# Neighbourhood attention in a fixed order with scores one block ahead, K laid out contiguously, and later differences in two Strassen MLPs

## The chip, the cores and the metric

The kernel runs on one core of one Trainium2 chip. Its engines are TensorE (PE, matrix products, with its weight loads shown as PEld), VectorE (DVE), ScalarE (ACT), GpSimd (POOL) and SyncE (SP), which here issues nearly all DMAs. The metric is device time in microseconds (us) from start to end of one execution; a comparison uses the median of several runs. A profile is one further execution, taken by the hardware profiler; all its times are counted from the start of its span.

## The reference

A trunk of two residual layers over 1024 tokens of width 1024, in float32. Layer 0 is neighbourhood attention and an MLP; layer 1 is a gated DeltaNet and an MLP. The change touches the attention and the first product of both MLPs:

```python
def sq_relu_mlp(h, w1, w2):
    a = jax.nn.relu(h @ w1)
    return (a * a) @ w2                      # width 4096 between the two

def neighbourhood_attention(h, w_qkv, rpb, w_o):
    ...                                      # 16 heads of 64, token grid 16 rows x 64 columns
    qkv = (h @ w_qkv).reshape(B, rows, GRID_W, 3, H, dh)
    ...                                      # window of 8 rows x 16 columns around each query
    bias = rpb[:, drow[None, :, None, :, None], dcol[:, None, :, None, :]].astype(jnp.float32)
    s = jnp.einsum('brjchd,bnjkhd->bhjrcnk', qb, kb).astype(jnp.float32) * scale + bias
    p = jax.nn.softmax(jnp.where(mask, s, -jnp.inf), axis=(-2, -1)).astype(vb.dtype)
    o = jnp.einsum('bhjrcnk,bnjkhd->brjchd', p, vb)
    ...
    return (o @ w_o).astype(h.dtype)
```

## The kernel before

Dense products run in three passes: a float32 operand is split into a rounded part `hi` (a copy on ACT) and a remainder `lo` (a subtraction on DVE), and `hi*hi`, `hi*lo` and `lo*hi` are summed in one bank of PSUM. `split_w` (lines 122 to 128) does this for 4 x 128 x 128 weights, which `wraw` and a DMA on SP bring in. `product` (L147) is one output tile of 128 x 512: eight inner tiles, 24 matmuls.

**The attention.** `load_x` loads the tokens in an order that puts each strip of 8 columns x 16 rows together: block t is 128 tokens. It also makes V for all heads. `na` then goes through eight pairs of heads. For a pair it makes K and then Q, feature-major (128 features of two heads x 1024 tokens): for each half of the tokens a `product`, a scaling out of PSUM on DVE (L694), the `hi` parts on ACT (L696, L703), the `lo` parts on DVE and POOL (L699, L704), and DMAs from POOL's queue (L698, L705) that bring the parts of either head to the other 64 partitions. `khi` holds K's `hi` part; `ks` and `qs` hold, for each head, a `hi` and a `lo` part one above the other, so that scores take two matmuls: one on 64 rows (`qs` on `khi`) and one on 128 rows (`qs` on `ks`), both on L726.

The scores of a block reach over its own and the neighbouring blocks (`nb` is 3, or 2 at the edges), so they are 128 x 384 or 128 x 256. K is read with the index order (row, block, column), that is in runs of 8 columns, since the bias table `bias` is laid out as 16 rows x 56 columns. One DVE operation adds the bias, negates and takes the minimum (L729); ACT takes the exponential with its sum (L732), and writes it in the order (block, row, column); DVE takes the reciprocal and scales (L736, L737). PE transposes the probabilities (L740), the two heads' transposes are copied by ACT and DVE (L743, L745), and output products with V (L750) fill 64 columns for each head. `load_bias` fetches the table of a pair with 32 DMAs (L676), for the next pair into the other two of four buffers; the table in DRAM, `natab`, is made by `na_bias_table`.

The order of this stage is not fixed by the text: a scheduler orders each engine's instructions by priority and by when their operands come. The DeltaNet of layer 1 is different: it runs within `manual_schedule`, where every engine keeps the order of the text. What comes before and behind such a stretch can still be placed among its instructions.

**The MLPs** are one level of Strassen's scheme (seven products instead of eight). `mlp_first` goes through quads of two hidden tiles by two halves of the tokens; a quad is seven products of twelve matmuls each (L430), in the order 1, 5, 2, 6, 3, 7, 4. After a product, DVE forms its sums (L418), ACT applies ReLU and square (L406, L407), and the hidden tile goes to DRAM. `less` (L411 to L415) forms at once the four differences that the second product needs, two of them in place over a hidden tile that has just been stored, and stores them in `diff`. `split` (L381, L382) prepares the weights of the product after next. `square_sum` loads a half tile of the residual stream and, two products later, squares it for the norm. `mlp_second` and `Second` do the second product.

Of the kernel before, what the change touches and what calls it, by code (L numbers as in the profile page):

```python
# [37 lines left out]
class Trunk:  # L38
# [302 lines left out]
    def mlp_first(self, st, w1, get, spare, first, todo, second, moved):  # L341
# [45 lines left out]
        def quad(n):  # L387
# [23 lines left out]
            def less(i, out, x, y):  # L411

                if n < nq - 4:
                    nc.vector.tensor_tensor(out=out, in0=x, in1=y, op=ALU.subtract)
                    nc.sync.dma_start(out=self.diff[n, i], in_=out)  # L415

# [41 lines left out]
        quads, shared, s, sq, w = [quad(n) for n in range(nq)], {}, {}, {}, {}  # L458
# [11 lines left out]
        for m, (n, j) in enumerate(order):  # L470
# [81 lines left out]
    def na_bias_table(self, rpb):  # L552

        nc = self.nc
        tab = self.dram.tile([16, 8, 15, 56], FP32, name="natab")
        for g in range(2):
# [7 lines left out]
            for h in range(8):  # L564
                nc.sync.dma_start(out=tab[8 * g + h].rearrange("q r k -> r q k"), in_=e[15 * h:15 * h + 15])
# [95 lines left out]
    def na(self, st, v, wqkv, rpb):  # L661
# [4 lines left out]
        for i in range(4):  # L666
            b = self.work(f"bias{i}", [P, 16, 56])
# [3 lines left out]
        def load_bias(n):  # L671
            for hh in range(2):
                for r in range(16):
                    r0 = min(max(r - 4, 0), 8)
                    d0 = 7 + r0 - r
                    nc.sync.dma_start(out=bias[n % 2 * 2 + hh][r * 8:r * 8 + 8, r0:r0 + 8, :], in_=tab[2 * n + hh, :, d0:d0 + 8, :])  # L676

        load_bias(0)
        o = []
        for n in range(8):  # L680


            khi = self.work("qk2", dt=F32R)
            ks = [self.work("wvraw", bufs=2, dt=F32R) for _ in range(2)]
            qs = [self.work(f"qk{i}", dt=F32R) for i in range(2)]
            ab = slice(0, 64), slice(64, 128)
            for c0, scale in ((D, 1.0), (0, 0.125)):
                w = self.weight(wqkv[:, c0 + n * P:c0 + (n + 1) * P])
                full = self.work("qk3") if c0 else None
                for half in range(2):  # L690
                    sl = slice(half * HALF, (half + 1) * HALF)
                    ps = self.product(w, x, half)
                    f = full[:, sl] if c0 else self.half("r")
                    nc.vector.scalar_tensor_tensor(out=f, in0=ps, scalar=scale, in1=st["rstd", half], op0=ALU.mult, op1=ALU.mult)  # L694
                    if c0:
                        nc.scalar.copy(out=khi[:, sl], in_=f)  # L696
# [1247 lines left out]
```

## Time and profile before

| | us |
|---|---|
| median of 3 runs | 2745.16 (2743.61 to 2745.78) |
| the profiled execution | 2742.01 |
| its span, first to last instruction | 2740.3 |
| mean granted TensorE clock | 0.989 |
| attention, first score to last output product | 138.0 to 524.4 |
| first product of MLP 0, its matmuls (L430) | 604.6 to 930.8 |
| first product of MLP 1, its matmuls (L430) | 2042.1 to 2383.1 |

In the rows of the profile, `mm<-X,whi` means that the tile `mm` is written from `X` and `whi`. A row of a timeline has the start, the time, the engine, the line, the operation and how many neighbours were merged; in brackets stands the idle time before it and what ended it. Matmuls are pipelined: one lasts about 0.4 us, and the next begins long before that, so the cost of one is read from start to start, not from its duration. A row of a table of stretches has the length, then busy time and count for PE, PEld, DVE, ACT and POOL, then the granted clock, the DMA share and GB/s. A row of waits has the total, the count and the longest.

### The profile page before, as it was taken

What the parts mean: (1) busy time and instruction counts of PE and PEld (TensorE: products, weight loads), DVE (VectorE), ACT (ScalarE), POOL (GpSimd) and SP (SyncE); (2) the same over time, 40 slices, a digit from 0 to 9 for tenths busy, and PEclk for the clock granted to TensorE, in tenths of its full rate; (3) what the DMA queues carried; (4) which work ended last, traced back from release to release, by engine and by line L of the source; (5) the groups of instructions that cost most, each with busy time, mean ns of one, the idle gap of its engine ahead of it and who ended that gap; (6) DMA issues with size and microseconds to landing.
All of it is one profiled execution on the core that took longest, in us unless ns stands there. A gap on an engine that the chain in (4) does not pass through costs nothing. (4 is left out here: it accounts for less than half of the span.)

```text
span 2740.3 us, 40418 instructions
## 1 busy us (share of the span) xinstructions
PE 2636.6 (96%) x14172; PEld 2072.7 (76%) x14172; DVE 1834.1 (67%) x3407; ACT 1293.2 (47%) x2747; POOL 939.5 (34%) x1067
## 2 busy tenths in 40 slices
PE   8999999999999999999999999898988999999998
PEld 6766666677788887787777878787866788888776
DVE  5156555665665667975777887878576665567975
ACT  5134344435555654433445555555354455554444
POOL 0111101025433422542345555533324543432641
PEclk9999999999999999999999999999999999999999
DMA  7222212346554543333221222123366544553334
GB/s 193 54 49 51 65 43 52 90 145 217 175 171 138 189 157 124 99 115 101 50 48 41 53 55 51 38 49 105 114 212 194 189 156 165 171 165 118 108 108 142
DMA packets 322233, 312.48 MB, mean 114 GB/s; under 512 B 81518, under 2 KB 233710, under 8 KB 322030
## 3 DMA queue, kind: packets, MB, share of 16 engines
q1 hardware_dynamic: 313614, 301.43, 36.2%
q0 software_dynamic: 3072, 8.39, 1.4%
q8 instruction: 111, 1.82, 0.3%
q10 hardware_dynamic: 5344, 0.09, 0.1%
q14 instruction: 92, 0.75, 0.1%
HBM read 209.78 MB, written 91.66 MB: 110 GB/s over the span
## 5 line engine op out<-in xcount | busy, mean ns | idle before, releaser
L1615 PE MATMUL mm<-A,whi 128*128 128x512 f32 x1216 | 405.3, 414 | 1.1 <-DVE A L1615 1.1
L147 PE MATMUL mm<-X,whi 128*128 128x512 f32 x1024 | 337.9, 402 | 0.7 <-ACT X L757 0.7
L1615 PEld LDWEIGHTS mm<-A,whi 128*128 128x128 f32 x1216 | 215.0, 191 | 41.2 <-DVE A L1615 1.9
L1615 PE MATMUL mm<-A,wlo 128*128 128x512 f32 x608 | 241.5, 397 | 0.0
L147 PEld LDWEIGHTS mm<-X,whi 128*128 128x128 f32 x1024 | 190.6, 188 | 47.5 <-issue 7.5
L147 PE MATMUL mm<-X,wlo 128*128 128x512 f32 x512 | 205.8, 402 | 0.0
L1615 POOL TENSOR_TENSOR xt<-lp,xi 128x126 f32<-128x126 f32 (+22 forms) x248 | 110.0, 444 | 175.4 <-DMA lp<-dsc 156.6
L1615 DVE SCALAR_TENSOR_TENSOR X<-xp,cw,X 128x512 f32<-128x512 f32 x192 | 141.7, 778 | 1.7 <-ACT X L1615 1.0
L1615 PEld LDWEIGHTS mm<-A,wlo 128*128 128x128 f32 x608 | 115.4, 190 | 28.1
L382 DVE TENSOR_TENSOR wlo<-s,whi 128x512 fp32r<-128x512 f32 x112 | 91.2, 819 | 56.6 <-ACT whi L381 56.6
L406 ACT ACTIVATE r<-r 128x512 f32<-128x512 f32 x120 | 75.7, 631 | 105.2 <-DVE r L418 105.1
L127 ACT CAST whi<-wraw 128x512 fp32r<-128x512 f32 (+1 forms) x110 | 66.0, 603 | 113.4 <-PE mm L147 77.2
L1615 POOL TENSOR_TENSOR xi<-xi,xt 128x126 f32<-128x126 f32 (+22 forms) x248 | 112.0, 451 | 19.4
L147 PEld LDWEIGHTS mm<-X,wlo 128*128 128x128 f32 x512 | 96.4, 188 | 20.6 <-issue 1.7
L128 DVE TENSOR_TENSOR wlo<-wraw,whi 128x512 fp32r<-128x512 f32 (+1 forms) x110 | 93.4, 851 | 27.0 <-ACT whi L127 26.9
L147 PE MATMUL mm<-A,whi 128*128 128x512 f32 (+1 forms) x336 | 105.7, 396 | 5.8 <-DVE hr L316 3.3
L1591 PE MATMUL mm<-X,whi 128*128 128x512 f32 x336 | 105.9, 396 | 0.0
L1591 PE MATMUL mm<-A,whi 128*128 128x512 f32 x336 | 105.9, 396 | 0.0
L1591 PE MATMUL pq<-X,whi 128*128 128x512 f32 x336 | 105.7, 396 | 0.0
L1591 PE MATMUL pq<-A,whi 128*128 128x512 f32 x336 | 105.7, 396 | 0.0
L698 POOL DMA_DIRECT2D wvraw<-qk x32 | 17.2, 540 | 247.0 <-ACT qk L696 240.4
L430 PE MATMUL pq<-X,whi 128*128 128x512 f32 x304 | 97.2, 401 | 0.0
(441 smaller groups left out, 7051.7 us busy)
## 6 DMA issues: line engine op xcount, KB each, us to landing
quad<-in_mlp_w_dram SPq DMA_DIRECT2D x60, 512.0 KB
hidden<-r SPq DMA_DIRECT2D x120, 256.0 KB
diff<-r SPq DMA_DIRECT2D x66, 256.0 KB
wraw<-in_gdn_w_in_dram SPq DMA_DIRECT2D x64, 256.0 KB
X<-in_mlp_w_dram SPq DMA_DIRECT2D x26, 512.0 KB
wraw<-in_mlp_w_dram SPq DMA_DIRECT2D x52, 256.0 KB
A<-in_mlp_w_dram SPq DMA_DIRECT2D x26, 512.0 KB
X<-diff SPq DMA_DIRECT2D x48, 256.0 KB
```

What stands on the lines that cost most here:

```text
L127: nc.scalar.copy(out=hi[:, :nk], in_=raw[:, :nk])
L128: nc.vector.tensor_tensor(out=lo[:, :nk], in0=raw[:, :nk], in1=hi[:, :nk].bitcast(FP32), op=ALU.subtract)
L147: nc.tensor.matmul(out=ps, lhsT=a, rhs=b[:, sl], start=n == 0, stop=n == last)
L382: nc.vector.tensor_tensor(out=lo, in0=left, in1=hi.bitcast(FP32), op=ALU.subtract)
L406: nc.scalar.activation(out=t, in_=t, func=AF.Relu)
L430: nc.tensor.matmul(out=ps, lhsT=u[:, i], rhs=x[:, v:v + HALF], start=i == 0 and m == 0, stop=i == 3 and m == 2)
L698: nc.gpsimd.dma_start(out=ks[i][ab[1 - i], sl].bitcast(FP32), in_=khi[ab[i], sl].bitcast(FP32))
L1591: nc.tensor.matmul(out=ps, lhsT=u[:, i], rhs=x[:, v:v + HALF], start=i == 0 and n == 0, stop=i == 3 and n == 2)
L1615: r = f(*args, **kw)
```

## The change

In the attention:

- `bias` and `natab` get the block index outside and the row inside, so that K, the scores and the probabilities are all in the order (block, row, column), and K is read without gaps.
- The heads move to a new function `na_heads` within `manual_schedule`. The dense products of the next pair become a generator; one `step()` is one inner tile, three matmuls. Q and K come in four parts: Q half 0, K half 0, K half 1, Q half 1. The weights come in six loads for a pair rather than four, since the two loads for Q are made again for its second half.
- Scores, reduction and exponential of a block are emitted one block ahead. A block's text is: transposes of both heads, next scores of head one, a step, next scores of head two, a step, a step, reciprocals and scalings of the next block, output products, a step. Weight splits lie in the steps 1, 5, 9, 21, 25 and 29 of the 32 of a pair; the eviction of a part comes in three pieces, in blocks 3, 4, 7 and, for the last part, block 0 of the next pair.
- K's second subtraction moves from POOL to DVE. In the last pair, the earlier pairs' outputs are split one in each block.

In the MLPs, `less` puts its subtraction and store on a list that is worked off behind the next product's operations, and `square_sum` loads behind products 1 and 6 and squares behind 2 and 7, where it was 5 and 3, and 6 and 4.

```diff
@@ mlp_first
-            if 2 <= n < 2 + ND and j in (5, 6, 3, 4):
-                half = j in (3, 4)
-                if j in (5, 3):
+            if 2 <= n < 2 + ND and j in (1, 2, 6, 7):
+                half = j in (6, 7)
+                if j in (1, 6):
...
             def less(i, out, x, y):
-                if n < nq - 4:
+                def form():
                     nc.vector.tensor_tensor(out=out, in0=x, in1=y, op=ALU.subtract)
                     nc.sync.dma_start(out=self.diff[n, i], in_=out)
+                if n < nq - 4:
+                    later.append(form)
...
+            ready, later[:] = list(later), []
             next(quads[n], None)
+            for f in ready:
+                f()
@@ na_bias_table
-        tab = self.dram.tile([16, 8, 15, 56], FP32, name="natab")
+        tab = self.dram.tile([16, 8, 7, 15, 8], FP32, name="natab")
@@ na
-            b = self.work(f"bias{i}", [P, 16, 56])
+            b = self.work(f"bias{i}", [P, 7, 16, 8])
...
+        with self.tc.manual_schedule(engines=ENGINES):
+            return self.na_heads(st, x, v, wqkv, bias, load_bias)
@@ na_heads
+    PARTS = (("q", 0), ("k", 0), ("k", 1), ("q", 1))
...
+        def split(m):
+            if m < 48:
+                ws[m] = self.split_w(raws.pop(m))
+                load(m + 3)
+
+        def dense():
+            for n in range(8):
+                for p in range(4):
+                    ps = banks[n, p] = self.ps.tile([P, HALF], FP32, tag="mm", name=self.uid("mm"), bufs=2)
+                    sl = slice(self.PARTS[p][1] * HALF, (self.PARTS[p][1] + 1) * HALF)
+                    for k in range(ND):
+                        at = {1: 1, 5: 2, 9: 3, 21: 4, 25: 5, 29: 6}.get(8 * p + k)
+                        if at:
+                            split(6 * n + at)
+                        whi, wlo = ws[6 * n + (0, 2, 2, 4)[p] + k // 4][k % 4]
+                        xhi, xlo = x[k]
+                        for i, (a, b) in enumerate(((whi, xhi), (whi, xlo), (wlo, xhi))):
+                            nc.tensor.matmul(out=ps, lhsT=a, rhs=b[:, sl], start=k == 0 and i == 0, stop=k == ND - 1 and i == 2)
+                        yield
+
+        def evict(n, p):
+            which, half = self.PARTS[p]
+            sl, f, ps = slice(half * HALF, (half + 1) * HALF), full[:, p % 2], banks.pop((n, p))
+            nc.vector.scalar_tensor_tensor(out=f, in0=ps, scalar=0.125 if which == "q" else 1.0, in1=st["rstd", half],
+                                           op0=ALU.mult, op1=ALU.mult)
+            yield
+            if which == "k":
+                nc.scalar.copy(out=khi[:, sl], in_=f)
+            else:
+                for i in range(2):
+                    nc.scalar.copy(out=qs[i][ab[i], sl], in_=f[ab[i]])
+            yield
+            for i in range(2):
+                if which == "k":
+                    nc.gpsimd.dma_start(out=ks[i][ab[1 - i], sl].bitcast(FP32), in_=khi[ab[i], sl].bitcast(FP32))
+                    nc.vector.tensor_tensor(out=ks[i][ab[i], sl], in0=f[ab[i]], in1=khi[ab[i], sl].bitcast(FP32), op=ALU.subtract)
+                else:
+                    nc.vector.tensor_tensor(out=f[ab[i]].bitcast(F32R), in0=f[ab[i]], in1=qs[i][ab[i], sl].bitcast(FP32), op=ALU.subtract)
+                    nc.gpsimd.dma_start(out=qs[i][ab[1 - i], sl].bitcast(FP32), in_=f[ab[i]])
+
+        def scores(n, t, hh):
...
+                nc.tensor.matmul(out=sps[:, :w], lhsT=qt[:, t * P:(t + 1) * P], rhs=kt[:, b0 * P:b1 * P], start=i == 0, stop=i == 1)
...
+            nc.scalar.activation(out=e[:, :w], in_=r[:, :w], func=AF.Exp, scale=-1.0, bias=nm, accum_out=sm)
+            def rest():
+                nc.vector.reciprocal(out=rc, in_=sm)
+                nc.vector.tensor_scalar(out=e[:, :w], in0=e[:, :w], scalar1=rc, scalar2=None, op0=ALU.mult)
+            return rest, (e, b0, b1 - b0)
...
+        for m in range(3):
+            load(m)
+        split(0)
+        for p in range(4):
+            for _ in range(ND):
+                step()
+            for _ in evict(0, p):
+                pass
         load_bias(0)
...
+                p = {3: 0, 4: 1, 7: 2}.get(t)
+                if p is not None and n < 7:
+                    left = evict(n + 1, p)
+                elif t == 0 and n:
+                    left = evict(n, 3)
+                nxt = []
+                for hh in range(2):
+                    if (n, t) != (7, 7):
+                        nxt.append(scores(n + (t == 7), (t + 1) % 8, hh))
+                    step()
+                next(left, None)
+                step()
+                next(left, None)
+                for rest, _ in nxt:
+                    rest()
+                for j in range(nb):
+                    for hh in range(2):
...
+                step()
+                next(left, None)
...
+                if n == 7 and t < 7:
+                    hi, lo = self.pair("X", t)
+                    nc.scalar.copy(out=hi, in_=o[t])
+                    nc.vector.tensor_tensor(out=lo, in0=o[t], in1=hi.bitcast(FP32), op=ALU.subtract)
+                    y.append((hi, lo))
```

More of the change, by code (lines that the diff above doesn't have):

```diff
@@ L456, in quad @@
                 second.prepare(n - nq, j)
-        quads, shared, s, sq, w = [quad(n) for n in range(nq)], {}, {}, {}, {}
+        quads, shared, s, sq, w, later = [quad(n) for n in range(nq)], {}, {}, {}, {}, []
         lead = "001010101001" if moved else "010101010001"
@@ L678, in na @@
         load_bias(0)
-        o = []
+        o, y, left = [], [], iter(())
+        now = [scores(0, 0, hh) for hh in range(2)]
+        for rest, _ in now:
+            rest()
         for n in range(8):
[L683 to L696, printed above, removed]
-                        for i in range(2):
-                            nc.gpsimd.dma_start(out=ks[i][ab[1 - i], sl].bitcast(FP32), in_=khi[ab[i], sl].bitcast(FP32))
-                            (nc.gpsimd if i else nc.vector).tensor_tensor(
-                                out=ks[i][ab[i], sl], in0=f[ab[i]], in1=khi[ab[i], sl].bitcast(FP32), op=ALU.subtract)
-                    else:
-                        for i in range(2):
-                            nc.scalar.copy(out=qs[i][ab[i], sl], in_=f[ab[i]])
-                            nc.vector.tensor_tensor(out=f[ab[i]].bitcast(F32R), in0=f[ab[i]], in1=qs[i][ab[i], sl].bitcast(FP32), op=ALU.subtract)
-                            nc.gpsimd.dma_start(out=qs[i][ab[1 - i], sl].bitcast(FP32), in_=f[ab[i]])
@@ L706, in na @@
             if n < 7:
                 load_bias(n + 1)
-            if n < 7:
                 on = self.slot(f"A{n}")
@@ L759, in na @@
-        y = []
-        for n in range(7):
-            hi, lo = self.pair("X", n)
-            nc.scalar.copy(out=hi, in_=o[n])
-            nc.vector.tensor_tensor(out=lo, in0=o[n], in1=hi.bitcast(FP32), op=ALU.subtract)
-            y.append((hi, lo))
+            for t in range(8):
+                if t % 4 == 0:
+                    ops = self.bank("o", [P, HALF], 2)
+                pts = []
+                for hh, (_, (e, b0, nb)) in enumerate(now):
+                    tps = self.bank("pt", [P, HALF], 2)
+                    for j in range(nb):
+                        nc.tensor.transpose(out=tps[:, j * P:(j + 1) * P], in_=e[:, j * P:(j + 1) * P], identity=self.ident)
+                    pts.append(self.half("r2")[:, :nb * P])
+                    (nc.vector.tensor_copy if hh else nc.scalar.copy)(out=pts[hh], in_=tps[:, :nb * P])
+                p = {3: 0, 4: 1, 7: 2}.get(t)
[12 more added lines that the diff above has]
+                for rest, _ in nxt:
+                    rest()
+                for j in range(nb):
+                    for hh in range(2):
+                        c = (2 * n + hh) * 64
+                        nc.tensor.matmul(out=ops[64 * hh:64 * hh + 64, (t % 4) * P:(t % 4 + 1) * P],
+                                         lhsT=v[b0 + j][:, c:c + 64], rhs=pts[hh][:, j * P:(j + 1) * P],
+                                         start=j == 0, stop=j == nb - 1)
+                step()
+                next(left, None)
+                if t % 4 == 3:
+                    sl = slice((t // 4) * HALF, (t // 4 + 1) * HALF)
+                    if n < 7:
+                        nc.scalar.copy(out=on[:, sl], in_=ops)
+                    else:
+                        nc.scalar.copy(out=y7[0][:, sl], in_=ops)
+                        nc.vector.tensor_tensor(out=y7[1][:, sl], in0=ops, in1=y7[0][:, sl].bitcast(FP32), op=ALU.subtract)
+                if n == 7 and t < 7:
[3 more added lines that the diff above has]
+                    y.append((hi, lo))
+                now = nxt
```

74 lines of the change are left out of this document (27 added, 47 removed).

## The prediction

> **What bounds the kernel now.** First the page, then a table of stretches.
>
> ```profile
> span 2740.3 us, 40418 instructions
> PE 2636.6 (96%) x14172; PEld 2072.7 (76%) x14172; DVE 1834.1 (67%) x3407; ACT 1293.2 (47%) x2747; POOL 939.5 (34%) x1067
> ```
> ```profile
> 150.00:500.00 350.00, 349.71 (x1839) 234.77 (x1837) 207.01 (x612) 152.19 (x374) 47.80 (x70) 1.00 0.20 50
> 850.00:900.00 50.00, 50.00 (x216) 40.36 (x215) 24.24 (x37) 26.34 (x44) 17.34 (x13) 1.00 0.37 121
> ```
>
> PE is busy from 150 to 500 us, the heart of the attention, and in a dense stretch of the MLP. The dense row gives one product of 512 columns: 50.0 / 216 = 0.232 us. The attention row says only that PE never waits; what its time goes into is seen from the starts of neighbours in PE's timeline. The rows by tile say where the stage begins and ends.
>
> ```profile
> L740 PE MATMUL pt<-ident,e x352: 270/272/329, 145.0 to 523.2; 128*128 128x128 f32 x176
> ```
> ```profile
> L726 PE MATMUL pa<-qk,qk x128: 384/439/451, 138.0 to 517.6; 64*128 64x384 f32 x96, 64*128 64x256 f32 x32
> ```
> ```profile
> L750 PE MATMUL o<-r,A x704: 272/273/324, 146.0 to 524.4; 128*64 128x128 f32 x176
> ```
> ```profile
> 250.12 0.40 PE L147 MATMUL mm<-X,whi 128*128 128x512 f32 x1
> 250.45 0.43 PE L750 MATMUL o<-r,A 128*64 128x128 f32 x2
> 250.81 0.55 PE L740 MATMUL pt<-ident,e 128*128 128x128 f32 x3
> 251.29 0.44 PE L726 MATMUL pa<-qk,qk 64*128 64x384 f32 x1
> 251.66 0.45 PE L726 MATMUL pa<-wvraw,qk 128*128 128x384 f32 x1
> 251.95 0.40 PE L147 MATMUL mm<-X,whi 128*128 128x512 f32 x1
> ...
> 253.26 0.87 PE L750 MATMUL o<-r,A 128*64 128x128 f32 x10
> 254.06 0.55 PE L740 MATMUL pt<-ident,e 128*128 128x128 f32 x3
> ```
>
> From first score to last output product: 138.0 to 524.4, 386 us. A dense product takes 0.33 instead of 0.232 when a 64-column product follows (250.12 to 250.45): leaving a shape costs 0.10. A score product of 384 columns is 0.29 (251.66 to 251.95) where 384 x 0.232 / 512 = 0.174 would do; it comes after a 64-row one, so entering a shape costs up to another 0.11 of exposed weights. Both changes together make the 0.37 of the 64-row product (0.174 + 0.10 + 0.10). So before, PE pays for changes of shape, not for waiting; a gain must come from fewer of them.
>
> **The change in the attention.** *K contiguous.* The working above leaves about 0.01 us for reading K in runs of 8 floats. Removing it saves nothing I can see (bound: 0.02 x 256 score products, 5 us); DVE and ACT work on as many elements as before. I take zero.
>
> *PE's work in a block.* A block is 128 queries (16 rows by 8 columns) of two heads. In the new order: six transposes, a score pair, three dense, a score pair, six dense, the output products, three dense. Transposes: 0.48 for three, with one exit and one entry, so 0.11 each, 0.66. Score pairs: 0.10 exit + 0.37 + 0.29 = 0.76, twice 1.52. Twelve dense: 2.78. Output products of the two heads fill half the columns each and start together: ten in 0.80 with entry and exit are 0.13 a pair if none ran alone; I take the 0.11 of a transpose. Three pairs, with entry 0.05, exit twice and the dense re-entry (0.30), make 0.68. Sum 5.64, and over a pair of heads 8 x 5.6 less 1.1 for the narrower first and last block: 43.7 us. Before it is near 386 / 8 = 48. Were PE the bound, this alone would save 30 us.
>
> *The wait it adds.* Now ACT and DVE also keep the order of the text. In six blocks of eight a weight split stands between the softmax of the next scores and its last step: ACT does both exponentials, then `whi`; DVE does both reductions, then `wlo`, which waits for `whi`, and only then the reciprocals and scalings (L736, L737) that the next transposes need.
>
> ```profile
> 300.91 0.56 DVE L745 COPY r<-pt 128x384 f32<-128x384 f32 x1 [0.26 <-PE pt L740]
> 301.38 0.41 DVE L737 TENSOR_SCALAR e<-e,rc 128x384 f32<-128x384 f32 x1
> 301.71 0.16 DVE L736 RECIPROCAL rc<-sm 128x1 f32<-128x1 f32 x1
> 301.78 0.54 DVE L729 CUSTOM_DVE_ANT_1 r<-pa,bias 128x384 f32<-128x384 f32 x1
> ...
> 302.25 0.42 DVE L737 TENSOR_SCALAR e<-e,rc 128x384 f32<-128x384 f32 x1
> 302.58 0.68 DVE L128 TENSOR_TENSOR wlo<-wraw,whi 128x512 fp32r<-128x512 f32 x1
> ```
> ```profile
> 300.96 0.62 ACT L732 ACTIVATE e<-r,nm 128x384 f32<-128x384 f32 x1 [0.97 <-ACT e L732]
> 301.48 0.19 ACT L732 ACTIVATION_READ_ACCUMULATOR e<-r,nm 128x1 f32 x1
> 301.57 0.60 ACT L127 CAST whi<-wraw 128x512 fp32r<-128x512 f32 x1
> ```
>
> The cycle from the second head's transposes to those of the next block: transposes 0.38, exit 0.10, first scores 0.66, dense 0.70, second scores 0.76 and 0.16 for the result to come out; reduction 0.04 + 0.55; exponential until `whi` may start 0.10 + 0.61; `whi` 0.60; `wlo` 0.03 + 0.60; then reciprocal and scaling of head one 0.19 + 0.33, of head two 0.19 + 0.42, and 0.06 to PE: 6.5 us against PE's 5.6. Without the split it is 4.8, and PE is the bound. So six blocks of a pair wait about 0.85 each, 5.2 in all. At the turn of a pair the two 64-row subtractions of the eviction (0.6 each on DVE, as from 698.94 to 699.55 below) stand before the next reduction: another 0.9. A pair costs 43.7 + 6.1 = 49.8. The wait is not in the trace of before; its bounds are 0 and 1.2 a block, and I take the worked 0.85.
>
> *What else moves.* A pair now loads and splits its two halves of the query weights twice: six loads and splits for four, 0.6 of ACT and of DVE each, counted above. The second K subtraction goes from POOL to DVE (0.6), inside the two counted at the turn. DVE sums to 16 x 0.87 for the softmax (0.46 + 0.33 + 0.08), 8 x 0.48 for copies, 12 x 0.6 for evictions, 6 x 0.6 for splits: 29 of 49.8, so its order costs, not its load. The bias tables travel in runs of 8 and of 64 floats; the DMA share of 0.20 in the row of 150 to 500 hides that, and 32 bias issues on SP (11 us, below) fit a pair, whose next weight load is needed 20 steps in.
>
> *The last pair* has no dense products left, so the chain alone sets it. Two rows more:
>
> ```profile
> L763 DVE TENSOR_TENSOR X<-A,X 128x1024 fp32r<-128x1024 f32 x7 | 8.5, 1221 | 1.1 <-ACT X L762 1.1
> L762 ACT CAST X<-A 128x1024 fp32r<-128x1024 f32 x7 | 7.0, 1047 | 5.0 <-PE mm L147 5.0
> ```
>
> Each block now carries one of these splits: exponential 0.61, cast 1.05, subtraction 1.14, copy of the transposes 0.48, two reductions 1.0, hand-overs 0.2: 4.5 us, some 35 for the pair. Its bubbles can take the first two products of `w_o` as far as seven of the eight pairs go (the two PSUM banks allow 42 matmuls); before they were hidden ahead of 524.4 as well, so I count them as free.
>
> *The head.* The biases of the first pair are loaded after nine weight loads on SP, the last of which waits for the seventh split, some 21 us behind the stage's first dense product (96 of them end at 138.0, so it starts near 115.7).
>
> ```profile
> 112.38 21.98 SPq L676 DMA_DIRECT2D bias<-natab  x64
> ```
> ```profile
> wvraw<-qk POOLq DMA_DIRECT2D x32, 128.0 KB, 2.6
> ```
>
> One issue is 21.98 / 64 = 0.34, so 32 end at 136.7 + 0.4 + 11 = 148; landing 2 (the nearest row has 2.6 for nine times the bytes), reduction 0.55, reciprocal and scaling 0.6: first transposes near 151, against 145.0 before. Sum: 151 + 7 x 49.8 + 35 = 534.6, ten us later than 524.4.
>
> *The clock.* PE then idles some 10 us at the head and runs thin in the last pair.
>
> ```profile
> 650.00:660.00 10.00, 8.36 (x29) 6.30 (x30) 6.29 (x9) 6.26 (x11) 5.84 (x4) 0.83 0.95 332
> ```
>
> A granted 0.83 over 10 us, behind a wait of 2.3 (below), is 3.4 us at half speed, 1.7 lost. Head one window, last pair one or two: 4 us (bounds 1 and 12). Attention in all: **+14** (bounds -29, no waits behind a split, and +25). The page "TensorE: Matmul & The Clock Gate" of the Trainium skill, section "What's actually happening", has the clock halved after an idle window of some 3.4 us; by that the head's idle time counts, but the last pair's bubbles of about 2 us do not, and the sum would be 2 us less. The row shows a shorter wait that was enough.
>
> **The change in the MLPs.** Before, a difference is formed at once, in DVE's order ahead of the next weight split.
>
> ```profile
> 696.23 0.71 DVE L414 TENSOR_TENSOR X<-r,r 128x512 f32<-128x512 f32 x1 [2.28 <-ACT r L407]
> 698.94 0.69 DVE L414 TENSOR_TENSOR r<-r,r 128x512 f32<-128x512 f32 x1 [2.01 <-DMA hidden<-r]
> 699.55 0.68 DVE L418 TENSOR_TENSOR r<-pq,X 128x512 f32<-128x512 f32 x1
> ```
> ```profile
> PE mm L430 <- DVE wlo L382: 5.3, 3, 2.9
> PE p L430 <- ACT whi L381: 2.3, 1, 2.3
> PE pq L430 <- DVE wlo L382: 1.1, 1, 1.1
> ```
> ```profile
> PE mm L430 <- DVE wlo L382: 6.6, 5, 2.4
> PE pq L430 <- DVE wlo L382: 4.7, 3, 2.0
> ```
> ```profile
> 625.00:725.00 100.00, 90.65 (x376) 70.25 (x375) 64.61 (x82) 52.84 (x95) 54.28 (x37) 0.98 0.66 212
> 2050.00:2175.00 125.00, 110.68 (x430) 84.41 (x429) 81.97 (x97) 58.17 (x105) 63.42 (x44) 0.93 0.61 193
> ```
>
> DVE waits first for ACT's square, then for the store of the hidden values it overwrites; PE's `wlo` stands behind. The waits on `wlo` (first fence 625 to 725, second 2050 to 2175) sum to 17.7 us. The whole loss by counts is 100 - 376 x 0.232 = 13 and 125 - 430 x 0.232 = 25: 38 us, slow clock included. One product later (12 x 0.232 = 2.8 us) the square is done and the store has mostly landed, since its longest wait was 2.01. I take four fifths of 17.7 (14) and a third of the rest (7): **-21**, bounds 0 and -33. The squares' loads moved to other products keep their distance of two products; they change what ACT waits for by a us or two either way, taken as zero; a load behind a pair of weight loads could cost 4.
>
> **Sum.** The profiled execution took 2742.0 (its span 2740.3 and 1.7 around it): 2742.0 + 14 - 21 = 2735. The median of the runs is 2745.2, 3.2 above it, so 2738.
>
> **Rivals.** *The split does not hold the block* (ACT or DVE is some 0.9 faster in the cycle, a contiguous exponential among the reasons): up to 43 us less, 2695; half of it 2716. For: DVE is idle over a us in the cycle. Against: each link is a row.
> *The last pair stays empty*: `w_o`'s dense products are not placed among the fixed instructions. Then 42 x 0.232 = 9.7 come after it, and PE, under half used, falls to half clock in most of its 35 us, +8: 2756, slower. It decides as soon as PE shows no L147 (`w_o`) before the last output product.
> *The MLP waits only move*: the later difference meets the same store and the next `wlo` stands behind it; half the gain goes: 2748, all of it: 2759.
>
> **How the numbers follow.** Forecast 0.50, split faster 0.30, within 0.16, slower 0.04, own range 2726 to 2750; fast attention 0.16, all faster; empty last pair 0.20 (faster 0.02, within 0.05, slower 0.13); moved waits 0.14 (faster 0.04, within 0.06, slower 0.04). Within 0.2% (2739.7 to 2750.6) is about what a measurement of this kernel cannot tell from no change. Faster 0.52, same 0.27, slower 0.21. The range 2711 to 2759 leaves out the fastest attention and the worst sum.
>
> **What would show it.** Per pair near 49.8 us; DVE idle before `wlo` for ACT's `whi` in six blocks of eight, and PE waiting there for the scaling; first transposes near 151; last output product near 535; no DVE wait for `hidden` ahead of a late `wlo` in the first quads. Wrong would be a pair near 44, a stage longer than 400 us, or MLP waits as before.

## The result, and the profile after

The changed kernel takes 2783.7 us, the median of four runs (2779.5 to 2786.3), against 2745.5 for the kernel before, also of four: a ratio of 1.0139, interval 1.0126 to 1.0152. It is 38 us slower. The forecast was 2738, the range 2711 to 2759: wrong, and on the wrong side.

The profiled execution took 2779.45 us. The page of the changed kernel opens with:

```profile
span 2777.4 us, 40318 instructions
PE 2636.3 (95%) x14172; PEld 2061.6 (74%) x14172; DVE 1854.3 (67%) x3439; ACT 1308.9 (47%) x2763; POOL 913.9 (33%) x1051
```

PE is busy for as long as before (2636.3 against 2636.6 us) in a span that is 37 us longer: the kernel gained idle time, not work. The rows by tile of the changed kernel, each with its first and last start, and two rows of its timeline (the copies of a finished half of a pair's output, one pair apart), say where:

```profile
L799 PE MATMUL pt<-ident,e x352: 270/273/476, 160.9 to 557.2; 128*128 128x128 f32 x176
L821 PE MATMUL o<-r,A x704: 272/273/476, 168.6 to 559.3; 128*64 128x128 f32 x176
```
```profile
264.09 0.58 ACT L829 COPY A<-o 128x512 f32<-128x512 f32 x1
...
314.59 0.58 ACT L829 COPY A<-o 128x512 f32<-128x512 f32 x1
```

| part, us of the trace | before | after | change |
|---|---|---|---|
| first transposes | 145.0 | 160.9 | +16 |
| from there to the last pair's transposes | 349.0 | 356.2 | +7 |
| last pair, to the last output product | 30.4 | 42.2 | +12 |
| first MLP, first product | 326.5 | 328.3 | +2 |
| second MLP, first product | 341.2 | 337.4 | -4 |
| all else | | | +4 |

A pair of heads now takes 50.5 us (264.09 to 314.59). The attention ends 35 us later, and the first products of the MLPs gain 2 us of the 21 forecast. The +4 of all else is spread over stages that the change doesn't touch; its cause stays open.

**The head.** The SP queue of the changed kernel, and its table of stretches (length, then busy time of PE, PEld, DVE, ACT and POOL with counts, granted clock, DMA share, GB/s):

```profile
136.01 44.72 SPq L682 DMA_DIRECT2D bias<-natab  x64
```
```profile
138.00:161.00 23.00, 0.81 (x4) 0.42 (x3) 2.90 (x9) 2.37 (x6) 1.03 (x2) 0.58 0.18 33
161.00:170.00 9.00, 8.93 (x28) 5.50 (x29) 3.75 (x12) 2.36 (x7) 0.00 (x0) 0.56 0.13 22
170.00:212.00 42.00, 41.44 (x232) 27.11 (x230) 23.74 (x70) 17.50 (x44) 2.06 (x4) 1.00 0.20 50
```

The 64 issues take 0.70 us each; the same 64 took 0.34 each before, and began at 112 instead of 136. PE is idle for 22 of the 23 us before the first transposes, and its clock is at half until 169 us, 8 us into the work that follows.

**A block with a weight split** in the changed kernel, on DVE, ACT and PE (start, length, and in brackets the idle time before it and what ended it):

```profile
299.12 0.56 DVE L759 CUSTOM_DVE_ANT_0 r<-pa,bias 128x384 f32<-128x384 f32 x1 [0.87 <-PE pa L756]
...
300.96 0.69 DVE L128 TENSOR_TENSOR wlo<-wraw,whi 128x512 fp32r<-128x512 f32 x1 [1.28 <-ACT whi L127]
301.57 0.15 DVE L765 RECIPROCAL rc<-sm 128x1 f32<-128x1 f32 x1
301.76 0.42 DVE L766 TENSOR_SCALAR e<-e,rc 128x384 f32<-128x384 f32 x1
```
```profile
299.72 0.62 ACT L762 ACTIVATE e<-r,nm 128x384 f32<-128x384 f32 x1 [0.73 <-DVE nm L759]
300.24 0.19 ACT L762 ACTIVATION_READ_ACCUMULATOR e<-r,nm 128x1 f32 x1
300.33 0.60 ACT L127 CAST whi<-wraw 128x512 fp32r<-128x512 f32 x1
```
```profile
300.41 0.88 PE L821 MATMUL o<-r,A 128*64 128x128 f32 x12
301.21 0.73 PE L727 MATMUL mm<-X,whi 128*128 128x512 f32 x2
301.78 0.40 PE L727 MATMUL mm<-X,wlo 128*128 128x512 f32 x1
302.33 1.04 PE L799 MATMUL pt<-ident,e 128*128 128x128 f32 x6 [0.16 <-DVE rc L765]
```

DVE stands 1.28 us for `whi`; only after `wlo` do the reciprocals and scalings run that the transposes at 302.33 wait for. The 0.16 in that row is only the time in which PE shows nothing: from the start of the product before (301.78) to the first transpose are 0.55 us, against 0.24 in a block with no wait. The chain is the one that the prediction worked out. Eight blocks of a pair take, from transposes to transposes, 6.91, 6.49, 6.48, 6.15, 5.93, 6.24, 5.95 and 6.36 us; 5.93 is a full block with no wait.

**The MLPs.** PE's waits from 560 to 970 us of the changed kernel (total us, times, longest) sum to 9.5 us, as before:

```profile
PE p L433 <- DVE wlo L382: 2.8, 4, 1.0
PE mm L433 <- DVE wlo L382: 2.1, 1, 2.1
PE p L433 <- ACT whi L381: 2.0, 1, 2.0
PE pq L433 <- DVE wlo L382: 1.7, 4, 0.7
PE pq L433 <- ACT whi L381: 0.9, 1, 0.9
```

One of them, followed back from PE to DVE and from DVE to ACT in the timeline:

```profile
715.72 0.50 PE L433 MATMUL mm<-A,wlo 128*128 128x512 f32 x1 [2.07 <-DVE wlo L382]
```
```profile
712.38 0.71 DVE L414 TENSOR_TENSOR X<-r,r 128x512 f32<-128x512 f32 x1 [2.25 <-ACT r L407]
713.01 0.68 DVE L421 TENSOR_TENSOR r<-pq,X 128x512 f32<-128x512 f32 x1
714.37 0.69 DVE L414 TENSOR_TENSOR r<-r,r 128x512 f32<-128x512 f32 x1 [0.68 <-DMA hidden<-r]
714.98 0.68 DVE L382 TENSOR_TENSOR wlo<-quad,whi 128x512 fp32r<-128x512 f32 x1
```
```profile
710.53 0.63 ACT L178 ACTIVATE sq<-sq 128x512 f32<-128x512 f32 x1 [2.50 <-DMA sq<-hs]
711.07 0.62 ACT L406 ACTIVATE r<-r 128x512 f32<-128x512 f32 x1
711.72 0.63 ACT L407 ACTIVATE r<-r 128x512 f32<-128x512 f32 x1
```

The deferred difference (L414 at 712.38) still waits for ACT's relu and square, and ACT had itself stood 2.50 us for the load of a square sum. The load, in turn, was issued at 707.22, when POOL's addition of the square before (705.90 to 707.19) had freed its one buffer. So this chain goes back to the square sums; the prediction had stopped at ACT's square of the hidden values.

### The profile page after: what moved, and what is told of

Same layout as the page of the kernel before. It is cut to its first block, busy times and chain, and to the rows that moved or that the text cites. A ratio compares the mean times of both kernels' runs of the same rounds, so it can differ in the third digit from the quotient of the medians.

```text
span 2777.4 us, 40318 instructions
## 1 busy us (share of the span) xinstructions
PE 2636.3 (95%) x14172; PEld 2061.6 (74%) x14172; DVE 1854.3 (67%) x3439; ACT 1308.9 (47%) x2763; POOL 913.9 (33%) x1051
## 5 line engine op out<-in xcount | busy, mean ns | idle before, releaser
L727 PE MATMUL mm<-X,whi 128*128 128x512 f32 x512 | 167.6, 409 | 0.0
L147 PE MATMUL mm<-X,whi 128*128 128x512 f32 x512 | 164.1, 401 | 0.0
L762 ACT ACTIVATE e<-r,nm 128x384 f32<-128x384 f32 (+1 forms) x128 | 75.4, 589 | 140.7 <-DVE nm L759 140.6
L127 ACT CAST whi<-wraw 128x512 fp32r<-128x512 f32 (+1 forms) x126 | 75.2, 601 | 108.8 <-PE mm L147 74.4
L382 DVE TENSOR_TENSOR wlo<-s,whi 128x512 fp32r<-128x512 f32 x112 | 85.4, 767 | 56.6 <-ACT whi L381 56.6
L759 DVE CUSTOM_DVE_ANT_0 r<-pa,bias 128x384 f32<-128x384 f32 (+1 forms) x128 | 66.9, 524 | 73.9 <-PE pa L756 52.5
L1665 PE MATMUL mm<-X,whi 128*128 128x512 f32 x336 | 105.8, 396 | 0.0
L1665 PE MATMUL pq<-X,whi 128*128 128x512 f32 x336 | 105.6, 395 | 0.0
```

Of the source, the lines that this page charges most:

```text
L127: nc.scalar.copy(out=hi[:, :nk], in_=raw[:, :nk])
L147: nc.tensor.matmul(out=ps, lhsT=a, rhs=b[:, sl], start=n == 0, stop=n == last)
L382: nc.vector.tensor_tensor(out=lo, in0=left, in1=hi.bitcast(FP32), op=ALU.subtract)
L727: nc.tensor.matmul(out=ps, lhsT=a, rhs=b[:, sl], start=k == 0 and i == 0, stop=k == ND - 1 and i == 2)
L759: nc.vector.tensor_tensor_reduce(out=r[:, :w], in0=sps[:, :w], in1=bias[n % 2 * 2 + hh][:, c0:c0 + b1 - b0].rearrange("p b r c -> p (b r c)"),
L762: nc.scalar.activation(out=e[:, :w], in_=r[:, :w], func=AF.Exp, scale=-1.0, bias=nm, accum_out=sm)
```

## The experiments

Times are medians; each ratio is to runs of the kernel before on the same chip in the same session (2742.5 to 2743.8 us). The first three runs divide the change into its parts.

**Attention alone** (the changed kernel with the MLP code of before, the diff below) and **MLPs alone** (the kernel before with the same diff the other way round):

```diff
-            if 2 <= n < 2 + ND and j in (1, 2, 6, 7):
+            if 2 <= n < 2 + ND and j in (5, 6, 3, 4):
...
-                def form():
+                if n < nq - 4:
                     nc.vector.tensor_tensor(out=out, in0=x, in1=y, op=ALU.subtract)
                     nc.sync.dma_start(out=self.diff[n, i], in_=out)
-
-                if n < nq - 4:
-                    later.append(form)
```

> The changed kernel with its attention, but the MLPs of before (differences formed at once, square sums in their old steps). Theory A (the MLP part of the change is worth nothing, the whole loss of 38 us is the attention's): 2784, within 4. Rival B (the MLP part saves the 21 us of the prediction, and the attention loses nearly 60): 2804. The first products of the two MLPs would take 326 and 338 us, as in the profile before, against 328 and 334 in that of the changed kernel.

> The attention of before, with the MLP part of the change alone. Theory A: 2745, within 4; PE's waits for the two halves of the split weights stay at about 9.5 us in the first MLP and 14 in the second. Rival B: 2724, those waits gone.

Measured: 2784.6 us (ratio 1.0146, 1.0128 to 1.0163), and 2743.2 us (0.9999, 0.9988 to 1.0009). Theory A holds: all of the loss is the attention's, and the MLP part is worth nothing that can be measured.

**The old layout of bias and K** in the new fixed order:

```diff
-            b = self.work(f"bias{i}", [P, 7, 16, 8])
+            b = self.work(f"bias{i}", [P, 16, 56])
...
-                nc.tensor.matmul(out=sps[:, :w], lhsT=qt[:, t * P:(t + 1) * P], rhs=kt[:, b0 * P:b1 * P], start=i == 0, stop=i == 1)
+                kv = kt[:, b0 * P:b1 * P].rearrange("p (b r c) -> p r b c", b=b1 - b0, c=8)
+                nc.tensor.matmul(out=sps[:, :w], lhsT=qt[:, t * P:(t + 1) * P], rhs=kv, start=i == 0, stop=i == 1)
```

> The changed kernel in its fixed order, but bias, K and exponentials in the layout of before (K read with a stride, bias rows of 1792 bytes). Theory A (the new bias layout, with runs of 256 bytes, doubles the time that SP needs to issue each bias transfer and so makes the head longer): 32 issues of 0.34 instead of 0.70 us, first transposes 11 us earlier at about 150, half speed of the clock for less time, 2784 - 11 to 16 = 2768 to 2773; a steady pair stays at 50.5 us. Rival C (reading K in one run is what the PE gains, so the strided read costs): a pair of 50.5 becomes longer by over 0.5 us. Rival D (issue time does not depend on the layout; the head is late because the order puts the bias behind the weights): 2784, first transposes still at 161.

Measured: 2772.1 us (1.0106, 1.0086 to 1.0126), 12 us less than the changed kernel; first transposes at 152.1. On SP, in this run:

```profile
138.26 22.60 SPq L682 DMA_DIRECT2D bias<-natab  x64
```

One issue takes 0.35 us again. The bytes are the same; before, each of a transfer's 8 partitions gets one run of 1792 bytes, and in the new layout seven of 256. So the layout doubles the issue time, and the place in the queue, behind the weights, makes the rest of the delay. A pair takes 51.1 instead of 50.5 us: half a microsecond more, 4 us in all, which is rival C's size but not its reason. It is not PE's reading of K: a block with no wait takes 5.94 us here and 5.93 in the changed kernel; the excess is in blocks with waits, and which link of their chain got longer stays open.

**The splits behind the scalings**, two steps later:

```diff
-                        at = {1: 1, 5: 2, 9: 3, 21: 4, 25: 5, 29: 6}.get(8 * p + k)
+                        at = ({3: 1, 7: 2, 11: 3, 23: 4, 27: 5, 31: 6} if n else {1: 1, 5: 2, 9: 3, 21: 4, 25: 5, 29: 6}).get(8 * p + k)
```

> The changed kernel with the weight splits of pairs 1 to 7 issued two steps later, behind the scalings of the next block's scores and the output products, instead of ahead of them. Theory A (in the six blocks with a split, the second scaling waits behind the low half of the split, which waits for ACT, and the transposes wait for it): the blocks of 6.2 to 6.9 us fall to the 5.9 of a block without a wait, the pair from 50.5 to about 47.4, seven pairs 20 us, 2784 - 20 = 2764, within 6. Rival E (PE's own work sets the pair): pair 50.5 and 2784. Rival F (the split is then late for the dense step that needs it, next in PE's order): PE waits for the high or the low half in place of the scaling, 2784 or more.

Measured: 2751.7 us (1.0022, 1.0011 to 1.0033), 32 us less. Its copies one pair apart, its stretch of one pair, and a stretch of one pair of the changed kernel:

```profile
258.07 0.57 ACT L829 COPY A<-o 128x512 f32<-128x512 f32 x1
...
304.17 0.57 ACT L829 COPY A<-o 128x512 f32<-128x512 f32 x1
```
```profile
304.00:351.00 47.00, 47.00 (x266) 32.28 (x266) 32.67 (x92) 22.80 (x56) 4.99 (x10) 1.00 0.28 67
```
```profile
314.00:365.00 51.00, 48.23 (x260) 31.02 (x260) 32.46 (x94) 22.54 (x55) 4.13 (x8) 1.00 0.26 62
```

A pair takes 46.1 us, its middle blocks, with and without a split, 5.92 to 5.93, and PE is busy without a gap. The split's place in two queues cost 4.4 us a pair. DVE and ACT do the same operations in both; only their order differs. In the traces, the stretch from the first transposes to those of the last pair falls from 356 to 327 us; the attention ends 25 us earlier (534.2 against 559.3), since its first transposes come at 162.4 and its last pair takes 45.1 us. The 46.1 is also 3.4 below the 49.5 us of a pair in the kernel before (its copies at 276.71 and 326.23). PE does the same products in both and stands still in neither, so the gain lies in the order in which they follow one another, fewer changes of shape by the prediction's account; the splits had hidden it.

**The first bias transfers spread** over the first pair's dense steps, one behind each:

```diff
-            for _ in range(ND):
+            for k in range(ND):
                 step()
+                i = 8 * p + k
+                load_bias(0, (i // 16,), (i % 16,))
...
-        load_bias(0)
```

> The changed kernel with the 32 bias transfers of the first pair issued one by one between the dense steps of that pair, instead of all behind them; nothing else. Theory A (the head's 16 us are SP's issue time of 0.70 us a transfer, and the idle that it gives PE sets its clock to half for 27 us): issue is done when the dense products end, first transposes at 141 to 142 instead of 161, no 27 us at half speed, first block 6.5 instead of 9.2 us: 2784 - 21 = 2763, within 5. Rival G (the bias rows land late for another reason, the table's own way through DRAM): first transposes still over 155, 2784.

Measured: 2761.9 us (1.0079, 1.0057 to 1.0101), 22 us less. First transposes are at 145.3, not 141: at one issue a step the last of the 32 ends near 142, and DVE stands 2.58 us, to 144.35, for the rows to land. The size came out right (22 us against 21) though two of its parts did not: the transposes are 4 us late, and 10 us at half speed are left.

**Both repairs**:

> The changed kernel with both repairs: splits two steps later, first bias transfers spread over the first pair's dense steps. Theory A: the two losses are apart in time and add: 2752 - 21 = 2731, within 5, against 2744 of the kernel before: ratio 0.995. Rival: the gains overlap through the clock, 2740 or more.

Measured: 2735.0 us (0.9977, 0.9965 to 0.9989). The two add to within 5 us, and the changed kernel so repaired is 0.2% faster than before, not the 0.5% expected.

**The output splits behind the last pair**, with both repairs:

```diff
-                if n == 7 and t < 7:
-                    hi, lo = self.pair("X", t)
...
                 now = nxt
+        for t in range(7):
+            hi, lo = self.pair("X", t)
...
```

> The changed kernel with both repairs, and the splits of the heads' outputs behind the loop of the last pair instead of one in each block. Theory A: no output-projection product can then run in the last pair, which falls from 42 to about 34 us; the 41 products of 0.23 us come back behind it: net 0 to -4, 2731 to 2735. Rival: the last pair's blocks stay at 5 us or more, as their own chain (scores, exponential, scaling) sets them without anything to fill, and the products come on top: 2740 or more.

Measured: 2736.6 us (0.9970, 0.9960 to 0.9981), the same as with them inside. The last pair falls from 42.2 to 32.9 us, as theory A says, but the products of `w_o` come back behind it: the first MLP begins at 597.2 instead of 595.6 us. So the length of the last pair alone is no measure of its cost.

**No loads for the square sums**, with differences at once and with differences later. The sums are taken over a resident tile, so they are of other values:

```diff
-                    nc.sync.dma_start(out=sq["t"], in_=self.hs[n - 2][:, half * HALF:(half + 1) * HALF])
...
-                    self.sumsq(n - 2, int(half), sq["t"], st, sq["t"])
+                    self.sumsq(n - 2, int(half), x[:, :HALF].bitcast(FP32), st, sq["t"])
```

> The kernel before, with the MLPs' running square sums taken over a tile that is resident (a left factor's slice) instead of over the stream loaded back for it: the loads are left out, so the sums are of other values; ACT and POOL do the same number of operations. Differences are formed at once, as before. Theory H (ACT, which works in order, stands behind these loads for some 2.5 us each, 30 us in the first MLP's first product; relu, squares and the weights' splits come late, and PE waits): PE's waits for the weights' halves fall from 9.5 and 14 us by more than half and the time by 10 to 20, to 2724 to 2734. Rival I (ACT has slack for it, and PE's waits come from DVE's own queue): 2744, within 4.

> The same with the MLP part of the change (differences one step later). Theory H with the deferral of use once ACT is not late: 5 or more below the run with differences formed at once. Theory H with the deferral of no use: equal to it within 3. Rival I: 2743, within 4, like the MLP part alone.

Measured: 2742.9 us (1.0000, 0.9990 to 1.0011) and 2743.6 us (1.0005, 0.9993 to 1.0018). By the time, theory H fails. The stretches of the first of the two show something else:

```profile
606.00:660.00 54.00, 45.12 (x169) 32.28 (x168) 34.98 (x36) 29.53 (x52) 39.76 (x28) 0.94 0.43 135
660.00:735.00 75.00, 75.00 (x322) 60.50 (x321) 48.67 (x66) 39.02 (x67) 28.71 (x20) 1.00 0.58 191
```

The first two quads take 13 us more than before (54.3 against 41.4 us to the first product of the third), and PE shows nothing for 8.9 of them; from then on it doesn't wait at all, with the differences formed at once as before. With no load to wait for, all 14 squares had run ahead into these quads (their starts lie between 616 and 648 us). There ACT, which has the weights' splits in the same queue, stood for POOL's additions (total us, times, longest):

```profile
ACT sq L178 <- POOL rs L179: 15.8, 13, 3.4
```

The 13 us lost there ate the 11 gained behind (273.8 against 285.1 us). So the experiment moved the cost rather than removing it, and the next pair of runs pins the squares.

**Square sums pinned**: over the quad's own finished results (loads left out, sums of other values), with differences at once (the diff) and later (there the square is of `c11` behind product 2 and of `c22` behind product 7):

```diff
-                    self.sumsq(n - 2, int(half), sq["t"], st, sq["t"])
+                    self.sumsq(n - 2, int(half), own, st, sq["t"])
...
-                square_sum(n, j)
+                square_sum(n, j, c11 if j == 6 else c21 if j == 4 else None)
```

> The kernel before (attention and differences as before), with the MLPs' square sums taken over the quad's own finished result, two a quad; the loads are left out, so the sums are of other values. Unlike in the run with a resident tile, the squares can't run ahead into the first two quads. Theory J (the waits of PE behind the first two quads, 9.7 and 8.8 us, come from ACT standing for the loads of the square sums, not from the differences): first products of 41 + 274 = 316 and 54 + 274 = 328 us instead of 326 and 341, the time 20 us less, 2724, within 5. Rival K (it is the squares and POOL's additions themselves, which take ACT and slow DVE): the waits stay, 2744. Rival L (the first two quads grow again by what the rest gains, something else bounds the stage): 2744, with the rest at 274.

> The same with the MLP part of the change (differences one step later, squares in the steps that it gives them). If theory J holds, the differences cost PE nothing wherever they stand: equal to the run before within 3. If the deferral is worth what was predicted once the loads are out of the way: 5 to 10 below it.

Measured: 2713.4 us (0.9885, 0.9871 to 0.9900) and 2710.6 us (0.9873, 0.9858 to 0.9887). The first products take 313.5 and 322.1 us in the first run, 313.6 and 322.4 in the second: theory J, with 9 us more than expected. The two times differ by less than their intervals, so the differences cost nothing that can be measured wherever they stand.

**Squares on POOL**, with both repairs and the loads:

```diff
-            nc.scalar.activation(out=sq, in_=hv, func=AF.Square)
+                nc.gpsimd.tensor_tensor(out=sq, in0=hv, in1=hv, op=ALU.mult)
```

> The changed kernel with both repairs, and the MLPs' squares taken by POOL instead of ACT, so that POOL stands for the loads and ACT does not; the values are the reference's. Theory J: the waits of PE behind the first two quads go at least by half, 2735 - 10 to 18 = 2717 to 2725. Rival M (POOL, which forms the sums of weights for the next quad, is then late by the loads and by a second operation of 1.3 us, and DVE slows beside it): 2735 or more.

Measured: 2749.7 us (1.0027, 1.0016 to 1.0038), 15 us more than with squares on ACT: rival M's number. POOL now stands for the loads, ACT doesn't, and PE's waits for `wlo` are still there:

```profile
POOL sq L181 <- DMA sq<-hs: 20.8, 8, 3.6
```
```profile
PE mm L436 <- DVE wlo L385: 9.3, 3, 4.5
```

But rival M's late sums of weights are not what the two longest of these waits, 4.5 and 2.9 us, go back to. It is a difference that DVE forms in place and that stands for a store of hidden values. For the second of them, DVE's row and two of SP's:

```profile
670.16 0.69 DVE L417 TENSOR_TENSOR r<-r,r 128x512 f32<-128x512 f32 x1 [4.39 <-DMA hidden<-r]
```
```profile
668.49 0.32 SPq L375 DMA_DIRECT2D sq<-hs  x1
668.86 0.42 SPq L411 DMA_DIRECT2D hidden<-r  x1
```

The values to store were ready at 667.1. The store was issued behind the next load of a square sum, and SP had stood for that load's one buffer until POOL's addition ended at 668.46. In this MLP, SP stands 48.2 us for that buffer, against 30.0 with the squares on ACT.

**The square written into a dead temporary of the quad**, with all loads kept. `p1` is dead after product 6 and again after product 4, so the square can't be placed before them; and with the square written elsewhere, the load's one buffer is free for the next load three to four products ahead of that one's square:

```diff
-            if 2 <= n < 2 + ND and j in (1, 2, 6, 7):
-                half = j in (6, 7)
-                if j in (1, 6):
+            if 2 <= n < 2 + ND and j in (1, 6, 3, 4):
+                half = j in (3, 4)
+                if j in (1, 3):
...
-                    self.sumsq(n - 2, int(half), sq["t"], st, sq["t"])
+                    self.sumsq(n - 2, int(half), sq["t"], st, dead)
...
-                square_sum(n, j)
+                square_sum(n, j, p1 if j in (6, 4) else None)
```

It ran with both repairs; with these and the first bias transfers two a step; and alone on the kernel before (differences at once).

> The changed kernel with both repairs in the attention, and each square of the MLPs written into a temporary of the quad that is dead by then, so that it can't run ahead of the quad; its load is asked for from three to four products earlier. All loads are kept, the values are the reference's. Theory J (the MLPs' loss is ACT standing for these loads, not the loads or squares themselves): the first products fall from 327 and 340 to about 315 and 325 us, 2735 - 27 = 2708, within 6. Rival N (the runs without loads were faster because the loads' traffic and issues were gone): 2730 or more, PE's waits behind the first two quads still 7 us or more.

> The same, with the first pair's bias transfers issued two behind each of the first 16 dense steps instead of one behind each of 32, so that the last is issued near 134 instead of 142. Theory A: the wait of the second scores for the bias is gone, first transposes at 142 instead of 146, and the 10 us at half speed behind them become none or a few: 4 to 9 us below the run before. Rival G (the weights' loads, queued behind two issues a step, then come late to the dense steps): PE waits there, no gain.

> The kernel before, with nothing changed but the squares of the MLPs, written as in the first run of this set; differences at once. Theory J: 2743 - 27 = 2716, within 6. Rival N: 2738 or more. Against the 27 us of the first run of this set it also tells what the later differences are worth beside it: equal gains mean nothing.

Measured: 2704.6 us (0.9859, 0.9841 to 0.9877), 2704.9 us (0.9866, 0.9845 to 0.9887) and 2713.8 us (0.9896, 0.9878 to 0.9913). The gain is 30 us with the later differences (2735.0 to 2704.6) and 29 without: with the loads in place, rival N is out. The first run beats both kernels. The same 75 us behind the first two quads, before, changed, and in this run, and the one wait that PE has left in this run's first MLP:

```profile
646.00:721.00 75.00, 67.67 (x279) 52.29 (x277) 46.00 (x59) 37.30 (x66) 38.56 (x28) 0.98 0.68 217
```
```profile
681.00:756.00 75.00, 66.37 (x267) 49.66 (x266) 43.84 (x57) 38.36 (x68) 38.45 (x28) 0.98 0.66 211
```
```profile
633.00:708.00 75.00, 75.00 (x324) 60.38 (x323) 49.99 (x68) 43.59 (x74) 35.25 (x25) 1.00 0.66 207
```
```profile
PE pq L433 <- DVE wlo L382: 0.3, 1, 0.3
```

324 products of 0.232 us fill the 75. DMA share and rate are close to those of before (0.66 and 207 GB/s against 0.68 and 217): the loads were never too many, their results were asked for too early. Two waits went together, though. With both repairs alone, ACT stands 32.3 us for these loads at its squares (L178) in the first MLP's first product, and SP 30.0 us for their buffer; in this run neither stands for them. No run takes away ACT's wait and leaves SP's as it was, so how the gain divides between the two is not shown; the run with squares on POOL, where ACT's was gone and SP's had grown, says that ACT's alone is not all of it.

The second run starts its transposes at 142.3 instead of 143.9 us and has 6.8 us at half speed instead of 10.2, but its time is the same, and the 4 to 9 us expected did not come. What is left of the head is a wait of 3.3 us on PE: on DVE the first reductions stand behind the eviction of Q's second half, until 140.6, and their own chain follows.

## Why the prediction was wrong

**The cycle of a split block: right, and decisive.** The prediction had each link and the wait; the run with the splits behind the scalings changed their place and nothing else, and 29 of the 356 us between the first transposes and the last pair's went. The wait was over-sized: 6.1 us a pair at 0.85 a block and the turn, measured 4.4 (50.5 less 46.1).

**PE's work in a block: under-sized.** Forecast 43.7 us a pair, measured 46.1. The step that failed is "ten in 0.80 ... Three pairs": the ten records of that row were not five output pairs. A block's text has six output products, three pairs, and the row above has twelve records of `o<-r,A` for it, so a pair leaves four records and ten were two and a half. The twelve take 0.80 us, from 300.41 to 301.21; with 0.10 for leaving the shape before and 0.10 for the slow entry behind (two dense products in 0.57 instead of 0.46) they cost 1.0 us, where I had 0.68. That is 0.3 us a block, the whole difference of 2.4. The two errors nearly cancel: 49.8 forecast, 50.5 measured.

**K contiguous at zero:** right for PE, whose strided reading costs nothing that shows in a block without waits (5.94 against 5.93 us). The layout as a whole was worth 0.5 us a pair, 4 in all, through blocks with waits.

**The head: mis-sized.** Forecast 151, measured 160.9. "One issue is 21.98 / 64 = 0.34" was read from the old layout and applied to the new one, though the change makes seven runs out of one. The prediction names these runs of 64 floats but asks only whether the DMAs have room for them, not what SP needs to issue them. That 32 issues at 0.70 are 22 us and not 11 accounts for the 10 us. For the clock I had one window here, 1.7 us lost. It was at half for 27 us, 19 of them idle, and the first block took 9.2 us instead of the 6.9 of later pairs.

**The last pair:** forecast 35, measured 42.2. The rival that it stays empty is false: 40 products of `w_o` start in it. The step that failed is the chain of 4.5 us a block: the full blocks without a wait take 4.9 to 5.1, and two stand in front of their transposes, for 1.76 and 1.46 us, and each time the clock falls behind it. The first of the two:

```profile
521.55 1.05 PE L799 MATMUL pt<-ident,e 128*128 128x128 f32 x6 [1.76 <-DVE rc L765]
```
```profile
517.00:523.00 6.00, 4.24 (x26) 2.46 (x24) 5.37 (x14) 4.73 (x11) 0.64 (x2) 1.00 0.28 69
523.00:528.00 5.00, 5.00 (x21) 2.99 (x21) 4.29 (x12) 2.39 (x6) 0.85 (x2) 0.66 0.32 75
```

At the second of them, a weight split of `w_o` stands in ACT's order ahead of the exponentials and in DVE's ahead of the reciprocals, the split block's mechanism again:

```profile
542.53 0.62 ACT L127 CAST whi<-wraw 128x512 fp32r<-128x512 f32 x1 [2.60 <-PE mm L147]
543.05 0.61 ACT L762 ACTIVATE e<-r,nm 128x384 f32<-128x384 f32 x1
```

By the page "TensorE: Matmul & The Clock Gate" of the Trainium skill, section "What's actually happening", an idle window of some 3.4 us halves the clock. Here a wait of 1.76 us was followed by 5 us at a granted 0.66, so the measurement stands against it, as the row in the prediction did. Of the 12 us that the last pair is longer than before, 4.4 are 19 more dense products in it (40 against 21, at 0.232), 2 are waits (3.2 us against 1.3) and 3.4 are what two stretches of 3.4 us at half speed lose; the other 2 stay open. None of it is won back behind: from the last output product to the first MLP it takes 80.8 us, and 80.2 before.

**The MLPs: forecast -21, measured nothing.** The step that failed is "PE's `wlo` stands behind" the differences. The row that it rested on said `[2.28 <-ACT r L407]`, and the cause was taken from DVE's queue without asking what ACT had waited for. In the trace of before, this stands in ACT's order ahead of that relu and square:

```profile
694.37 0.63 ACT L178 ACTIVATE sq<-sq 128x512 f32<-128x512 f32 x1 [2.45 <-DMA sq<-hs]
```

It waited for the loads of the square sums, of which the prediction said that moving them was "taken as zero". The changed kernel has these waits too (ACT's, in the first MLP; total us, times, longest):

```profile
ACT sq L178 <- DMA sq<-hs: 34.5, 14, 4.5
```

With them gone (squares pinned), the quads behind the second fall from 285.1 and 287.6 us to 273.7 each, waits and slow clock together, and the time by 29 us. The rival "the MLP waits only move: all of it" has the MLPs' number right, no gain, but for another reason: it still looked to the differences, and these cost nothing once the square sums are out of the way. Whether ACT's wait for the load or SP's for its buffer weighs more stays open.

**The sum.** Head 10 over the forecast, the pairs with the slow first block 8 over, the last pair 7 over: the last output product comes 25 us later than forecast (559.3 against 534.6). The prediction had added 4 us for the clock apart from that, so the attention is +35 instead of +14. The MLPs are -2 instead of -21. Forecast and result differ by 46 us: 21 in the attention, 19 in the MLPs, some 4 in all else, and 1 because the median lies 4.3 us above the profiled execution instead of 3.2.

## What to carry to other kernels

Where engines work in order, placing an operation early for the engine that needs it can put its wait ahead of work that another engine needs sooner: place it behind the chain that the block waits for. Follow a wait back until an engine that waited for nothing or a transfer is found, and for a transfer ask what kept it from being issued earlier; here a remedy for a link in the middle changed nothing. And price a transfer whose layout changes by its new runs, not by the row of the old one.

## What the hardware showed that was not expected

SP's time to issue one 14 KB transfer went from 0.35 us with one run of 1792 bytes in a partition to 0.70 with seven of 256, at equal bytes. After 22 us nearly without work, PE was still at half clock for 8 us of full work (161 to 169), where a wait of 1.76 us in the last pair was followed by 3.4 us at half (5 us at 0.66).
